# Ten raw weight tiles in place of eight, and another order of the seven block products in a two-layer trunk on one core

## Chip, core and metric

One Trainium2 chip, one core. The metric is the device time of one execution of the program in microseconds (us), where lower is better. The engines are TensorE (PE, matmuls), VectorE (DVE), ScalarE (ACT), GpSimd (POOL) and SyncE (SP, which here only issues DMAs). Each engine runs its own instructions in program order and waits on semaphores for the others.

## What is computed

The trunk has two layers on 256 tokens of width 2048, all in float32. The feed-forward half of each layer, where the change sits, is

```python
h = rms_norm(x, nw[2])
gate, up = jnp.split(h @ w_ffn_in[l], 2, axis=-1)      # 2048 x (2 * 5632)
x = x + rms_norm((jax.nn.silu(gate) * up) @ w_ffn_out[l], nw[3])
```

The other half projects `h` with `w_in` (2048 x 11264), runs a gated linear recurrence and a differential attention, projects both, merges them with sigmoid gates and projects again with `w_out`. Every weight is read once.

## The kernel before

**Weights.** Class `Weights` streams the weights as blocks of 256 x 512 float32 (512 KB). SP loads a block into a `w_raw` tile (L113). ACT casts it to the reduced type as `w_hi` (L130), and DVE forms the remainder `w_lo = w_raw - w_hi` (L131), called "the lo" of the block below. PE multiplies by each block three times (hi by the activations' hi, hi by their lo, lo by their hi): L365 to L367 in plain products, L454 to L456 in the fold groups. There are `RAW = 8` raw tiles, and `BUFS = 7` tiles each for hi and lo; conversion runs at most `LOOK = 5` blocks ahead of the block that PE asks for. A load is issued when a raw tile is free and at most `RAW - 1` blocks ahead of the block converted last.

**Fold groups.** Ten of the eleven 512-wide column pairs (gate, up) of each layer are computed by `fold_group`: for a 2 x 2 part of the blocks, seven products p1 to p7 stand in for eight, and the remaining blocks of both halves are multiplied plainly (A8, A10, A12, A14 for gate, B8 to B14 for up; "A12" is the block of rows 12 x 128 and following). Each product has two blocks, k0 and k1. The products need sums of weight blocks, made in place in the raw tiles: X starts as the block uA; after p1 has been converted, a DMA on POOL's queue adds uB to it from memory (`then`, L134, "X pair" for the two blocks), and p5 uses the sum. p6 adds Y on DVE (`plus`, L127), after which a second DMA pair adds uB to Y ("Y pair") for p7; p4 adds Z to X (`plus` again). So each group has four accumulating DMAs, 80 in all. Where such a DMA has not landed, the cast of the next use (p5 or p7) waits on ACT, and all of ACT's later casts behind it.

**Accumulators.** A fold group holds four PSUM tiles `s`, `b`, `c`, `d`, and there are only four, so that the next group's take over the same ones. `hold` (L1111, ACT) copies a finished `s`, `b` or `c` to SBUF: "hold p1", "hold p5", "hold u2", "hold p4". `out_a(0)` and `out_a(1)` (L1116, DVE) read `d` and `s` and give the gate; its sigmoid and product are L1092 (ACT) and L1093 (DVE). `out_b(0)` and `out_b(1)` (L1121, DVE) read `b` and `s` and give the up half, and L1096 (DVE) multiplies it in. PE's B8 for the second token tile writes `s` and so waits for `out_a(1)`; the next group's A8 writes what was `b` and waits for `out_b(0)`.

**Order.** The feed-forward is cut into four parts of 2, 3, 3 and 3 columns. In the first part one column is plain and one is a fold group ("alone" below, 2 in all); in the others each has three fold groups back to back, the first of which follows a plain stretch ("first", 6 in all) and the other two a fold group ("following", 12 in all). Between the parts come the plain products with `w_ffn_out`. While a group runs, the previous one's gated tile is transposed on PE (`hid`, L328 on DVE). PE runs its products in the order of the code. On DVE, ACT and SP the tile scheduler places each instruction, mostly by when the code asks for it. Within a group the blocks run in this order: p1 p1 A8 A10 p5 p5 p2 p2 p3 p3 p6 p6 A12 A14 p4 p4 p7 p7, then B8 B10 for the first token tile, B8 B10 for the second, B12 B14.

Of the kernel before, what the change touches and what calls it, by code (L numbers as in the profile page):

```python
# [12 lines left out]
F32 = mybir.dt.float32  # L13
F32R = mybir.dt.float32r
# [5 lines left out]
P = 128  # L20
# [6 lines left out]
NC = 512  # L27
KB = 2
# [40 lines left out]
class Weights:  # L69
# [2 lines left out]


    LOOK = 5
    RAW = 8
    BUFS = 7

    def __init__(self, nc, raw_pool, split_pool):
# [39 lines left out]
    def emit(self, upto):  # L118
        nc = self.nc
        upto = min(upto, self.oldest + self.BUFS - 1, len(self.order) - 1)  # L120
        while self.emitted <= upto:
            self.load(self.emitted)
            assert self.loaded > self.emitted
            key, _, plus, then, last = self.order[self.emitted]
            raw = self.raw[key]
            if plus is not None:
                nc.vector.tensor_tensor(raw, raw, self.raw[plus], op=ALU.add)  # L127
            hi = self.split_pool.tile([P, KB, NC], F32R, name="w_hi")
            lo = self.split_pool.tile([P, KB, NC], F32R, name="w_lo")
            nc.scalar.copy(hi, raw)  # L130
            nc.vector.tensor_tensor(lo, raw, hi.bitcast(F32), op=ALU.subtract)  # L131
            if then is not None:
                to, where = then
                nc.gpsimd.dma_start(self.raw[to], self.block(where), accum_op=ALU.add)  # L134
            for k in last if isinstance(last, tuple) else (key,) * last:
                del self.raw[k]
                self.live -= 1
            self.made[self.emitted] = (hi, lo)
            self.emitted += 1
            self.load(self.emitted + self.RAW - 1)  # L140

# [13 lines left out]
def hybrid_trunk(ctx: ExitStack, tc: tile.TileContext, ins, out):  # L155
# [22 lines left out]
        return work.tile([P, NC], F32, name=name, tag="w2")  # L178

    def stg_tile(name):  # L180
        return work.tile([P, NC], F32, name=name, tag="stg", bufs=7)

    def gate_tile(name):
        return work.tile([P, NC], F32, name=name, tag="stg", bufs=7)

    bg = Background()

# [222 lines left out]
    def fold_plan(src, nj, col_a, col_b, fold):  # L410
# [9 lines left out]
        ids = {}  # L420

        def through(col, ks):
            for k in ks:
                ids[col, k] = W.add(src=(src, k * P, col_a if col == "A" else col_b))
# [3 lines left out]
        through("A", plain[0:2])  # L428
        for i in n:
            ids["p5", i] = W.add(X[i], last=False)  # L430
        for i in n:
            ids["p2", i] = W.add(Z[i], dA[i], last=False)
        for i in n:
            ids["p3", i] = W.add(Y[i], dB[i], last=False)
        for i in n:
            ids["p6", i] = W.add(X[i], plus=Y[i], then=(Y[i], uB[i]), last=False)
        through("A", plain[2:])
        for i in n:
            ids["p4", i] = W.add(X[i], plus=Z[i], last=(X[i], Z[i]))
        for i in n:  # L440
# [4 lines left out]
    def fold_group(plan, lhs, hold, out_a, out_b):  # L445
# [12 lines left out]
        def folded(f, ps, first=False):  # L458
            for i in range(n):
                w = W.get(ids[f, i])  # L460
                for k in range(KB):
                    three(ps, lhs.factor[f, i, k], [s[:, k] for s in w], first and i == k == 0,
                          i == n - 1 and k == KB - 1)
                W.done(ids[f, i])
                bg.step()

        def through(col, k, ts, pss, first=False, done=True):
            w = W.get(ids[col, k])
            for t in ts:
                for i in range(KB):  # L470
                    three(pss[t], lhs.chunk(k + i, t), [s[:, i] for s in w], first and i == 0, i == KB - 1)
            if done:
                W.done(ids[col, k])
                bg.step()
# [4 lines left out]
            through("A", k, (0, 1), (d, c), m == 0)  # L479
        folded("p5", b, True)  # L480
        p5 = hold(b, 1.0)
        folded("p2", d)
        folded("p3", b)
        folded("p6", s)
        u2 = hold(s, 1.0)
        for k in plain[2:]:
            through("A", k, (0, 1), (d, c))
        out_a(0, p1, d, p1, ALU.add)
        folded("p4", c)
        p4 = hold(c, 1.0)  # L490
# [697 lines left out]
```

## Time and profile before

| what | value |
|---|---|
| median of 3 runs (lowest, highest) | 3014.52 us (3005.62, 3015.57) |
| the profiled execution, its span in the trace | 3015.97 us, 3014.2 us |
| PE busy | 2909.9 us, 97% of the span |
| DVE busy, ACT busy, POOL busy | 1936.3 us, 1451.9 us, 208.0 us |
| PE waiting for DVE at L454 (fold groups) | 75.6 us |
| bytes read from memory | 565.39 MB, 190 GB/s over the span |
| 20 fold groups in the trace | 945.7 us |

The profile is of one execution on the chip. "Busy" of PE counts a matmul's time whatever the clock, so a stretch at half clock looks as busy as one at full clock; the granted clock (1.00 is full speed) is read from the windows. A releaser in square brackets is what ended the idle time ahead of an instruction. DMA-issuing instructions of POOL stand as rows, and a DMA's landing is seen in who waited for it.

### The profile page before, as it was taken

Reading aid. Unit: us, or ns where it says so; the run is one execution under the profiler, and the core shown is the slowest. Engines: PE = TensorE matmul, PEld = TensorE weight load, DVE = VectorE, ACT = ScalarE, POOL = GpSimd, SP = SyncE. Lnnn points to the kernel's source line nnn. Section 1 sums busy time; section 2 is a strip of 40 time slices with the busy share of each in tenths; the row PEclk is TensorE's granted clock in tenths of the full one; section 3 lists DMA queues with packets and bytes.
Section 4 is the critical chain, followed back from the end, with each engine's and each line's share of the span. In section 5 each row is a group of like instructions: output and inputs, shape, how many; then the busy total and the mean of one; then the engine's idle time right before and its main releaser. Section 6 shows DMA issues by size and latency. Waiting matters only on the chain.

```text
span 3014.2 us, 35271 instructions
## 1 busy us (share of the span) xinstructions
PE 2909.9 (97%) x13194; PEld 2398.7 (80%) x13194; DVE 1936.3 (64%) x2098; ACT 1451.9 (48%) x1765; POOL 208.0 (7%) x236
## 2 busy tenths in 40 slices
PE   9999999999998998999999999999999999999988
PEld 7888888887786777877878888888877877777777
DVE  6676555555857667677666755455567676675775
ACT  6344544444655445455453444444445554454553
POOL 2002100000000000010000021000000010000000
PEclk9999999999999999999999999999999999999999
DMA  8555566665766776767665555666657767676674
GB/s 282 153 162 160 162 186 190 191 198 183 232 186 189 217 194 158 237 170 238 203 216 155 161 154 168 188 189 190 223 173 224 197 161 234 169 200 205 167 235 143
DMA packets 296315, 576.09 MB, mean 191 GB/s; under 512 B 18496, under 2 KB 18896, under 8 KB 296144
## 3 DMA queue, kind: packets, MB, share of 16 engines
q1 hardware_dynamic: 273232, 529.80, 55.3%
q0 software_dynamic: 21760, 41.95, 8.8%
q8 instruction: 103, 1.69, 0.2%
q10 hardware_dynamic: 1152, 2.10, 0.2%
q14 instruction: 68, 0.56, 0.1%
HBM read 565.39 MB, written 8.39 MB: 190 GB/s over the span
## 4 chain that ended last, share of the span: by engine, by line
PE 51%; issue 33%; DMA 8%; DVE 6%; ACT 1%; POOL 1%; POOLq 0%; SPq 0%; DVEq 0%; ACTq 0%
PE acc L365 13%; PE acc L367 13%; PE acc L366 13%; DMA w_raw<-in_w_ffn_in_dram 7%; DVE w_lo L131 4%; PE acc L454 3%; PE acc L455 3%; PE acc L456 3%; PE tp L630 2%; ACT w_hi L130 1%; PE tp L315 1%; DMA x_t<-in_x_dram 1%; POOL w_raw L134 1%; DVE w_raw L127 0%; DVE x_t L820 0%
## 5 line engine op out<-in xcount | busy, mean ns | idle before, releaser
L131 DVE TENSOR_TENSOR w_lo<-w_raw,w_hi 128x1024 fp32r<-128x1024 f32 x1128 | 1365.8, 1226 | 960.2 <-ACT w_hi L130 939.5
L130 ACT CAST w_hi<-w_raw 128x1024 fp32r<-128x1024 f32 x1128 | 1166.0, 1050 | 1357.1 <-PE acc L366 889.0
L365 PE MATMUL acc<-w_hi,xT 128*128 128x512 f32 x1536 | 616.7, 402 | 8.2 <-ACT w_hi L130 8.1
L367 PE MATMUL acc<-w_lo,xT 128*128 128x512 f32 x1536 | 603.5, 393 | 2.6 <-DVE w_lo L131 2.4
L366 PE MATMUL acc<-w_hi,xT 128*128 128x512 f32 x1536 | 601.5, 392 | 0.7 <-DVE xT L328 0.7
L454 PE MATMUL acc<-w_hi,xT 128*128 128x512 f32 x800 | 329.9, 412 | 75.5 <-DVE held L1116 44.7
L367 PEld LDWEIGHTS acc<-w_lo,xT 128*128 128x128 f32 x1536 | 289.9, 189 | 68.8 <-DVE w_lo L131 6.7
L365 PEld LDWEIGHTS acc<-w_hi,xT 128*128 128x128 f32 x1536 | 290.6, 189 | 65.6 <-ACT w_hi L130 9.8
L366 PEld LDWEIGHTS acc<-w_hi,xT 128*128 128x128 f32 x1536 | 290.9, 189 | 58.4 <-DVE xT L328 1.6
L455 PE MATMUL acc<-w_hi,xT 128*128 128x512 f32 x800 | 323.6, 405 | 0.0
L456 PE MATMUL acc<-w_lo,xT 128*128 128x512 f32 x800 | 323.0, 404 | 0.0
L366 PE MATMUL acc<-w_hi,hid 128*128 128x512 f32 x704 | 274.8, 390 | 0.0
L365 PE MATMUL acc<-w_hi,hid 128*128 128x512 f32 x704 | 274.4, 392 | 0.0
L367 PE MATMUL acc<-w_lo,hid 128*128 128x512 f32 x704 | 274.2, 390 | 0.0
L454 PEld LDWEIGHTS acc<-w_hi,xT 128*128 128x128 f32 x800 | 157.5, 197 | 122.1 <-DVE held L1116 52.7
L456 PEld LDWEIGHTS acc<-w_lo,xT 128*128 128x128 f32 x800 | 157.5, 197 | 34.9
L455 PEld LDWEIGHTS acc<-w_hi,xT 128*128 128x128 f32 x800 | 158.1, 198 | 32.5
L134 POOL DMA_DIRECT2D w_raw<-in_w_ffn_in_dram x80 | 97.5, 1219 | 1182.1 <-DVE w_lo L131 921.9
L366 PEld LDWEIGHTS acc<-w_hi,hid 128*128 128x128 f32 x704 | 132.2, 188 | 28.7 <-DVE hid L328 1.9
L367 PEld LDWEIGHTS acc<-w_lo,hid 128*128 128x128 f32 x704 | 132.1, 188 | 27.5
L365 PEld LDWEIGHTS acc<-w_hi,hid 128*128 128x128 f32 x704 | 132.2, 188 | 27.0
L454 PE MATMUL acc<-w_hi,fold_hi 128*128 128x512 f32 x320 | 125.7, 393 | 0.0
(204 smaller groups left out, 2920.9 us busy)
## 6 DMA issues: line engine op xcount, KB each, us to landing
w_raw<-in_w_in_dram SPq DMA_DIRECT2D x352, 512.0 KB, 3.8
w_raw<-in_w_ffn_in_dram SPq DMA_DIRECT2D x312, 512.0 KB, 4.8
w_raw<-in_w_ffn_out_dram SPq DMA_DIRECT2D x176, 512.0 KB, 4.8
w_raw<-in_w_ffn_in_dram POOLq DMA_DIRECT2D x80, 512.0 KB, 6.8
w_raw<-in_w_out_dram SPq DMA_DIRECT2D x64, 512.0 KB, 4.4
w_raw<-in_w_branch_a_dram SPq DMA_DIRECT2D x32, 512.0 KB, 3.6
w_raw<-in_w_branch_b_dram SPq DMA_DIRECT2D x32, 512.0 KB, 4.1
x_dram<-x_t SPq DMA_DIRECT2D x24, 256.0 KB, 5.5
```

The lines of the kernel that those rows point to most:

```text
L130: nc.scalar.copy(hi, raw)
L131: nc.vector.tensor_tensor(lo, raw, hi.bitcast(F32), op=ALU.subtract)
L134: nc.gpsimd.dma_start(self.raw[to], self.block(where), accum_op=ALU.add)
L315: nc.tensor.transpose(tp[:, i], src[:, i * P : (i + 1) * P], ident)
L365: nc.tensor.matmul(ps, xh, hi[:, j], start=first, stop=False)
L366: nc.tensor.matmul(ps, xl, hi[:, j], start=False, stop=False)
L367: nc.tensor.matmul(ps, xh, lo[:, j], start=False, stop=last)
L454: nc.tensor.matmul(ps, xh, hi, start=first, stop=False, skip_group_check=True)
L455: nc.tensor.matmul(ps, xl, hi, start=False, stop=False, skip_group_check=True)
L456: nc.tensor.matmul(ps, xh, lo, start=False, stop=last, skip_group_check=True)
L630: nc.tensor.matmul(ps[:, i, t], blk, right, start=True, stop=True)
```

## The change

There are ten raw tiles in place of eight. The room comes from the lo tiles (six in place of seven; the hi tiles stay seven) and from the tiles tagged `stg`, which hold the held and gated values (six in place of seven). In a fold group p2 moves from behind p5 to behind A14, and A12 moves from behind p6 to behind p5: p1 p1 A8 A10 p5 p5 A12 p3 p3 p6 p6 A14 p2 p2 p4 p4 p7 p7, and B as before. Lines behind the two functions move down by one or two: `hold` is L1113, `out_a` L1118, `out_b` L1123, the gated product L1098.

```diff
--- before.py
+++ after.py
@@ -72,7 +72,7 @@
 
 
     LOOK = 5
-    RAW = 8
+    RAW = 10
     BUFS = 7
 
     def __init__(self, nc, raw_pool, split_pool):
@@ -126,7 +126,7 @@
             if plus is not None:
                 nc.vector.tensor_tensor(raw, raw, self.raw[plus], op=ALU.add)
             hi = self.split_pool.tile([P, KB, NC], F32R, name="w_hi")
-            lo = self.split_pool.tile([P, KB, NC], F32R, name="w_lo")
+            lo = self.split_pool.tile([P, KB, NC], F32R, name="w_lo", bufs=self.BUFS - 1)
             nc.scalar.copy(hi, raw)
             nc.vector.tensor_tensor(lo, raw, hi.bitcast(F32), op=ALU.subtract)
             if then is not None:
@@ -178,10 +178,10 @@
         return work.tile([P, NC], F32, name=name, tag="w2")
 
     def stg_tile(name):
-        return work.tile([P, NC], F32, name=name, tag="stg", bufs=7)
+        return work.tile([P, NC], F32, name=name, tag="stg", bufs=6)
 
     def gate_tile(name):
-        return work.tile([P, NC], F32, name=name, tag="stg", bufs=7)
+        return work.tile([P, NC], F32, name=name, tag="stg", bufs=6)
 
     bg = Background()
 
@@ -428,13 +428,14 @@
         through("A", plain[0:2])
         for i in n:
             ids["p5", i] = W.add(X[i], last=False)
-        for i in n:
-            ids["p2", i] = W.add(Z[i], dA[i], last=False)
+        through("A", plain[2:3])
         for i in n:
             ids["p3", i] = W.add(Y[i], dB[i], last=False)
         for i in n:
             ids["p6", i] = W.add(X[i], plus=Y[i], then=(Y[i], uB[i]), last=False)
-        through("A", plain[2:])
+        through("A", plain[3:])
+        for i in n:
+            ids["p2", i] = W.add(Z[i], dA[i], last=False)
         for i in n:
             ids["p4", i] = W.add(X[i], plus=Z[i], last=(X[i], Z[i]))
         for i in n:
@@ -479,12 +480,13 @@
             through("A", k, (0, 1), (d, c), m == 0)
         folded("p5", b, True)
         p5 = hold(b, 1.0)
-        folded("p2", d)
+        through("A", plain[2], (0, 1), (d, c))
         folded("p3", b)
         folded("p6", s)
         u2 = hold(s, 1.0)
-        for k in plain[2:]:
+        for k in plain[3:]:
             through("A", k, (0, 1), (d, c))
+        folded("p2", d)
         out_a(0, p1, d, p1, ALU.add)
         folded("p4", c)
         p4 = hold(c, 1.0)
```

DVE, from the end of the fourth fold group to the first products of the fifth. In the list before, w_raw_8422 and 8424 are the new group's X blocks (so their first lo's are those of p1), and L1116 is the old group's `out_a(1)`:

```order
L131 TENSOR_TENSOR w_lo_8509<-w_raw_8409,w_hi_8508 128x1024
L131 TENSOR_TENSOR w_lo_8521<-w_raw_8422,w_hi_8520 128x1024
L131 TENSOR_TENSOR w_lo_8538<-w_raw_8424,w_hi_8537 128x1024
L1116 TENSOR_TENSOR held_8506<-held_8506,acc_8282 128x512
L131 TENSOR_TENSOR w_lo_8551<-w_raw_8436,w_hi_8550 128x1024
L1093 SCALAR_TENSOR_TENSOR held_8506<-held_8506,rs_5964,sgf_8534 128x512
L131 TENSOR_TENSOR w_lo_8573<-w_raw_8450,w_hi_8572 128x1024
```

and after, where 8417 and 8419 are the X blocks:

```order
L131 TENSOR_TENSOR w_lo_8513<-w_raw_8378,w_hi_8512 128x1024
L131 TENSOR_TENSOR w_lo_8523<-w_raw_8417,w_hi_8522 128x1024
L1118 TENSOR_TENSOR held_8510<-held_8510,acc_8284 128x512
L131 TENSOR_TENSOR w_lo_8538<-w_raw_8419,w_hi_8537 128x1024
L1095 SCALAR_TENSOR_TENSOR held_8510<-held_8510,rs_5966,sgf_8534 128x512
L131 TENSOR_TENSOR w_lo_8551<-w_raw_8432,w_hi_8550 128x1024
```

`out_a(1)` stood behind both lo's of the next p1, and now stands between them.

DVE, the rows that follow, from the second use of X (p5). Before, L1121 are `out_b(0)` and `out_b(1)` of the old group, 8498 and 8512 are Z (p2) and 8525 is the first Y block (p3):

```order
L131 TENSOR_TENSOR w_lo_8589<-w_raw_8422,w_hi_8588 128x1024
L127 TENSOR_TENSOR w_raw_8422<-w_raw_8422,w_raw_8525 128x1024
L131 TENSOR_TENSOR w_lo_8615<-w_raw_8424,w_hi_8614 128x1024
L1121 TENSOR_TENSOR held_8444<-acc_8283,held_8444 128x512
L127 TENSOR_TENSOR w_raw_8424<-w_raw_8424,w_raw_8542 128x1024
L1096 SCALAR_TENSOR_TENSOR held_8444<-held_8444,rs_5950,held_8308 128x512
L1121 TENSOR_TENSOR held_8364<-acc_8282,held_8364 128x512
L131 TENSOR_TENSOR w_lo_8627<-w_raw_8498,w_hi_8626 128x1024
L1096 SCALAR_TENSOR_TENSOR held_8364<-held_8364,rs_5964,held_8506 128x512
L131 TENSOR_TENSOR w_lo_8639<-w_raw_8512,w_hi_8638 128x1024
L131 TENSOR_TENSOR w_lo_8655<-w_raw_8525,w_hi_8654 128x1024
```

and after, where 8474 is A12's block and 8490 the first Y block:

```order
L131 TENSOR_TENSOR w_lo_8593<-w_raw_8417,w_hi_8592 128x1024
L127 TENSOR_TENSOR w_raw_8417<-w_raw_8417,w_raw_8490 128x1024
L1123 TENSOR_TENSOR held_8442<-acc_8285,held_8442 128x512
L1123 TENSOR_TENSOR held_8372<-acc_8284,held_8372 128x512
L1098 SCALAR_TENSOR_TENSOR held_8442<-held_8442,rs_5952,held_8308 128x512
L1098 SCALAR_TENSOR_TENSOR held_8372<-held_8372,rs_5966,held_8510 128x512
L131 TENSOR_TENSOR w_lo_8617<-w_raw_8419,w_hi_8616 128x1024
L131 TENSOR_TENSOR w_lo_8627<-w_raw_8474,w_hi_8626 128x1024
L131 TENSOR_TENSOR w_lo_8639<-w_raw_8490,w_hi_8638 128x1024
```

Both `out_b` stood behind the lo of p5's second block and now stand ahead of it; between that lo and p3's first there were seven instructions, and now there is one, A12's lo.

ACT in the fifth group, from p6 to p7. Before, L1111 held_8692 is hold p5 and held_8787 is hold u2; 8592 and 8618 are A12 and A14:

```order
L130 CAST w_hi_8681<-w_raw_8422 128x1024
L130 CAST w_hi_8695<-w_raw_8424 128x1024
L130 CAST w_hi_8714<-w_raw_8592 128x1024
L1111 ACTIVATE held_8692<-acc_8611 128x512
L130 CAST w_hi_8733<-w_raw_8618 128x1024
L327 CAST hid_8706<-tp_8707 128x4x128
L130 CAST w_hi_8746<-w_raw_8422 128x1024
L327 CAST hid_8706<-tp_8726 128x4x128
L130 CAST w_hi_8761<-w_raw_8424 128x1024
L130 CAST w_hi_8775<-w_raw_8525 128x1024
L1111 ACTIVATE held_8787<-acc_8610 128x512
L130 CAST w_hi_8789<-w_raw_8542 128x1024
```

and after, where 8542 is A14, 8554 and 8578 are Z (p2), held_8700 is hold p5 and held_8785 hold u2:

```order
L130 CAST w_hi_8687<-w_raw_8419 128x1024
L130 CAST w_hi_8702<-w_raw_8542 128x1024
L130 CAST w_hi_8728<-w_raw_8554 128x1024
L1113 ACTIVATE held_8700<-acc_8613 128x512
L130 CAST w_hi_8745<-w_raw_8578 128x1024
L327 CAST hid_8720<-tp_8721 128x4x128
L130 CAST w_hi_8756<-w_raw_8417 128x1024
L327 CAST hid_8720<-tp_8738 128x4x128
L130 CAST w_hi_8771<-w_raw_8419 128x1024
L130 CAST w_hi_8787<-w_raw_8490 128x1024
L130 CAST w_hi_8803<-w_raw_8502 128x1024
L1113 ACTIVATE held_8785<-acc_8612 128x512
```

Hold p5 stood behind A12's cast and now stands behind that of p2's first block; hold u2 stood ahead of the cast of p7's second block and now stands behind it.

At the program's start SP issues, before, three weight blocks, two tiles of x, six weight blocks, and the last tile of x; after, eight weight blocks stand ahead of that last tile of x in place of six. PE's products keep their order outside the fold groups.

## Rows read from the trace of the kernel before

**Rows 1.** The page, part 1: engine, busy us (share of the span), number of instructions.

```profile
PE 2909.9 (97%) x13194; PEld 2398.7 (80%) x13194; DVE 1936.3 (64%) x2098; ACT 1451.9 (48%) x1765; POOL 208.0 (7%) x236
```

**Rows 2.** PE's waits: instruction, what it waited for, us in total, times, longest.

```profile
PE acc L454 <- DVE held L1116: 44.7, 19, 4.9
PE acc L454 <- DVE held L1121: 26.8, 12, 4.4
PE acc L365 <- ACT w_hi L130: 8.1, 4, 2.2
PE acc L454 <- DVE hd L1096: 4.1, 2, 3.3
```

**Rows 3.** Timeline of PE: start, duration, line, in brackets idle time before and releaser.

```profile
1122.29 0.50 PE L454 MATMUL acc<-w_hi,xT 128*128 128x512 f32 x1 [3.19 <-DVE held L1116]
...
1138.72 0.50 PE L454 MATMUL acc<-w_hi,xT 128*128 128x512 f32 x1 [2.25 <-DVE held L1121]
```

**Rows 4.** Windows: length; PE, PEld, DVE, ACT, POOL busy (count); clock, DMA share, GB/s.

```profile
928.30:931.70 3.40, 3.37 (x8) 2.73 (x9) 3.40 (x4) 2.28 (x4) 0.00 (x0) 0.51 0.00 0
932.00:935.40 3.40, 3.40 (x16) 2.76 (x16) 3.40 (x4) 1.05 (x1) 0.25 (x1) 1.00 0.00 0
```

**Rows 5.** Line 134: duration in ns (min/median/max); its waiters (us, times); landing time.

```profile
L134 POOL DMA_DIRECT2D w_raw<-in_w_ffn_in_dram x80: 1203/1213/1381, 777.2 to 2907.2; - x80
...
  ACT w_hi L130: 211.1, 54
...
DMA to landing us min/median/max: 5.7/6.8/10.2
```

**Rows 6.** Timeline of ACT in the fifth group and the start of the sixth.

```profile
1135.76 3.90 ACT L130 CAST w_hi<-w_raw 128x1024 fp32r<-128x1024 f32 x4 [6.21 <-DMA w_raw<-in_w_ffn_in_dram]
...
1160.13 2.95 ACT L130 CAST w_hi<-w_raw 128x1024 fp32r<-128x1024 f32 x3 [2.00 <-DMA w_raw<-in_w_ffn_in_dram]
...
1185.16 3.89 ACT L130 CAST w_hi<-w_raw 128x1024 fp32r<-128x1024 f32 x4 [7.51 <-DMA w_raw<-in_w_ffn_in_dram]
```

**Rows 7.** Timeline of DVE in the same stretch (x4: four instructions in a row).

```profile
1136.84 1.23 DVE L131 TENSOR_TENSOR w_lo<-w_raw,w_hi 128x1024 fp32r<-128x1024 f32 x1 [4.77 <-ACT w_hi L130]
1137.99 0.68 DVE L1121 TENSOR_TENSOR held<-acc,held 128x512 f32<-128x512 f32 x1
...
1142.78 4.62 DVE L131 TENSOR_TENSOR w_lo<-w_raw,w_hi 128x1024 fp32r<-128x1024 f32 x4
```

**Rows 8.** Timeline of POOL in the same stretch: the accumulating DMAs.

```profile
1145.55 1.21 POOL L134 DMA_DIRECT2D w_raw<-in_w_ffn_in_dram  x1 [15.60 <-DVE w_lo L131]
1151.77 1.22 POOL L134 DMA_DIRECT2D w_raw<-in_w_ffn_in_dram  x1 [5.01 <-DVE hid L328]
1169.82 1.21 POOL L134 DMA_DIRECT2D w_raw<-in_w_ffn_in_dram  x1 [16.83 <-DVE w_lo L131]
```

**Rows 9.** Windows over the twelve following groups: the third of them, and the sum.

```profile
1132.23:1179.48 47.25, 43.97 (x189) 35.57 (x188) 35.71 (x36) 26.26 (x30) 4.87 (x4) 0.96 0.71 198
...
sum 586.48, PE 531.61 PEld 429.91 DVE 442.79 ACT 321.31 POOL 43.84; mean PE 44.30 PEld 35.83 DVE 36.90 ACT 26.78 POOL 3.65
```

**Rows 10.** The same over the six first groups: the second, the third, and the sum.

```profile
1086.30:1132.23 45.93, 42.74 (x182) 34.84 (x180) 33.97 (x32) 25.29 (x28) 4.87 (x4) 0.96 0.71 199
1295.43:1336.90 41.47, 41.09 (x181) 33.71 (x180) 34.07 (x32) 24.89 (x28) 4.84 (x4) 1.00 0.76 217
...
sum 267.42, PE 252.54 PEld 206.35 DVE 198.38 ACT 153.11 POOL 29.14; mean PE 42.09 PEld 34.39 DVE 33.06 ACT 25.52 POOL 4.86
```

**Rows 11.** The same over the two groups that stand alone: the first, and the sum.

```profile
787.55:832.46 44.91, 42.37 (x189) 34.42 (x188) 35.60 (x35) 27.32 (x31) 2.43 (x2) 1.00 0.72 220
...
sum 91.80, PE 86.00 PEld 70.05 DVE 73.16 ACT 54.63 POOL 4.85; mean PE 43.00 PEld 35.03 DVE 36.58 ACT 27.32 POOL 2.43
```

**Rows 12.** The start: timeline of PE, and a window over all engines.

```profile
22.84 0.63 PE L315 MATMUL tp<-ident,x_t 128*128 128x128 f32 x4 [0.96 <-DMA x_t<-in_x_dram]
...
8.00:22.00 14.00, 12.98 (x52) 9.57 (x52) 11.73 (x11) 8.58 (x11) 8.24 (x5) 1.00 1.03 372
```

## The prediction

> **What bounds the kernel now.** I read the page first: PE is busy 97% of the span [rows 1], so only its idle time and its slow time can be won. The view of PE's waits says where the idle time is: 44.7 us at L454 for L1116 in 19 waits and 26.8 us for L1121 in 12, and 4.1 us for the gated product [rows 2]. That is 75.6 us, all in the fold groups, and all for DVE. The timeline shows one of each: PE stands 3.19 us for `out_a(1)` and 2.25 us for `out_b(0)` [rows 3]. A wait costs more than its idle time: after one, 3.4 us run at clock 0.51 (the lower of the two levels, 1.2 GHz), with 8 matmuls where the next window has 16 at full clock [rows 4], so some 1.7 us are lost on top.
>
> DVE has no lack of time (64% busy [rows 1]), so the next question is what makes it late. Line 134's view answers: ACT waited 211.1 us in 54 waits for accumulating DMAs, which land 6.8 us after their issue in the median (5.7 to 10.2) [rows 5]. ACT is in order, so all later casts stand behind such a wait, and all of DVE's lo's behind the casts.
>
> The three timelines of the fifth and sixth group give a closed loop, from p5's second cast to the same cast one group later [rows 6 to 8]:
> (a) that cast starts at 1135.76; DVE forms its lo at 1136.84, then goes through `out_b` and its company from 1137.99 to 1142.78, then four lo's 1.14 apart, of which the second is p3's first, done at 1142.78 + 2 x 1.14 = 1145.06: 9.3 us.
> (b) The Y pair, issued at 1145.55 and, as the second goes out only when the first has landed, at 1151.77; the cast of p7's second block starts at 1160.13: 15.1 us.
> (c) Casts and lo's up to p1's first of the next group, whose X pair POOL issues at 1169.82, 0.45 us behind the lo's end: 9.2 us.
> (d) The X pair, until p5's second cast at 1185.16: 15.8 us.
> The sum is 49.4 us, and the twelve following groups last 586.48 / 12 = 48.87 us each [rows 9]. PE alone would need less: the third of the first groups ran at clock 1.00 almost without waits and took 41.47 us for its 180 matmuls, 0.23 each [rows 10]; eight transposes more raise PE's busy time from 41.09 to 42.37 us [rows 10, 11], so a following group needs between 41.5 and 42.7. Hence the loop is what sets the twelve groups' length, and PE's two waits are how it shows.
>
> **Following groups (twelve).** The new order takes six instructions from between the lo's of p5k1 and p3k0: both `out_b`, both gated products and one `plus` go ahead of p5k1's lo or behind p3k0's (the lists of DVE), and p2's two lo's give way to A12's one. Those ahead fill the time in which DVE waits for the X pair anyway (4.77 us idle there [rows 7], against 2.5 us of work). Part (a) becomes 1.08 us from cast to lo plus three lo's of 1.14, 4.5 us in place of 9.3, so 4.8 us less. Parts (b), (c), (d) hold the same instructions as before, so I leave them. The mean goes from 48.87 to 44.1 us, still above PE's 42.7 at most. Twelve times 4.8 is **57.6 us**. What is late next is the same loop, so I expect a wait of some 2 us per group at `out_a(1)` to stay, and the one at `out_b` to go, since `out_b` no longer stands behind a lo that waits for an accumulating DMA.
>
> **First groups (six).** They come to 267.42 us, or 44.6 each [rows 10], without part (d). Between the lo's of p5k1 and p3k0 stand two additions of the size of L1121's (0.6 us apart from the next row, 1137.99 [rows 7]), a `plus` as long as a lo, and p2's two lo's; A12's lo alone remains, which brings the Y pair forward by 3.5 us, and `out_a(1)` is one lo (1.14) earlier besides. Together 4.6 us against a wait of 3.19 us in the group shown [rows 3]; so I let the waits go and take 41.7 us, just above the undisturbed 41.47: 6 x 2.9 = **17 us**. The bounds are nothing, if these waits hang on something other than the lo's, and 18.6 us.
>
> **Groups alone (two).** 91.80 us [rows 11]; PE's own 42.4 each would save 7.0. Their wait for the gated product goes, since these too stand ahead of p5k1's lo. I take **7 us**, between 0 and 7.
>
> **Tiles.** Six lo tiles make DVE wait for the product six blocks back where the hi tiles wait for the seventh. In plain stretches a block is converted some five blocks ahead, so at most one block's PE time (2.8 us, 12 matmuls of 0.23) of a lead of some 14 us is lost; I cost it at nothing, covered by that lead. It moves the X pair of a first group some 1.6 us later, which lands before p5 all the same. Six tiles for held and gated values: four are live in a group and two wait for their transposes, so six do; nothing, and if a release came late it would hold ACT's hold, with casts queued behind it.
>
> **Start.** Ten tiles let SP issue two more weight loads ahead of the last tile of x. PE waits 0.96 us for that tile already [rows 12], and the DMA engines are full, at 372 GB/s; two loads of 524 KB take 1.05 MB / 372 GB/s = 2.8 us, all of it on the path: **+2.8 us**, with bounds of 0 and 3.
>
> **New waits.** On ACT, hold p5 now stands behind the cast of p2's first block, which waits for PE to finish p5 (seven hi tiles) and for the sums X += Y. By the first it ends 48 matmuls into the group, 11.0 us, plus a cast and the hold: 12.7 us. By the second, counting DVE's rows, it ends 10.3 us after p5k1's cast. PE writes the same accumulator again with p3, 60 matmuls or 13.8 us into the group, so hold p5 costs nothing while p5k1's cast starts within 3.5 us of the group's start; in the fifth group that was 1135.76 - 1132.23 = 3.5 us [rows 6, 9], and it should come down with part (a). I take nothing, with 0 to 2.2 us per group (the sixth group's cast, at 1185.16, came 5.7 us after its start). Hold u2, now behind the cast that waits for the Y pair, is needed only by p7, which needs that pair itself; nothing.
>
> **Sum.** The profiled execution took 3015.97 us, 1.45 us above the median of three. 3016.0 - 57.6 - 17.2 - 7.0 + 2.8 = 2937.
>
> A rule that bears on parts (b) and (d): the rows give 5.7 us at least from issue to landing for 512 KB [rows 5]. The Trainium skill, page "DMA: Bandwidth & Descriptors", section "Anatomy of one DMA — SWDGE (gpsimd) path", fits 2.0 us plus bytes over 436e3, an estimate of 3.2 us here. By that a pair would take about 7 us, the loop 33 before the change, PE would be the bound already, and the change would gain nothing in the following groups. The trace disagrees, as ACT's 54 waits show, and the sum goes by the trace.
>
> **Rivals.**
> 1. *All waits in the fold groups go.* This happens if the pairs get shorter too, as loads come earlier with ten tiles and leave the accumulating DMAs alone. For it: a landing of 5.7 us was seen; four of these in place of 6.8 take 4.4 us off the loop, down to 39.7, under PE. Against: loads go on at about 198 GB/s all through [rows 9]. Following groups 12 x (48.87 - 42.4) = 77.6, the others 18.6 + 7.0, start 2.8: 2916; with PE's 8.1 us of waits for hi in plain stretches [rows 2] gone as well, 2908.
> 2. *Part of the gain is taken back.* One landing of the four at 10.2 us in place of 6.8 makes the loop 47.5 us: 12 x 1.4 = 16 us in place of 57.6, so 2978. Or hold p5 becomes the late one: 2.2 us in each of twelve, 26 us, so 2963.
> 3. *Slower.* Ten tiles let SP put two more loads beside each accumulating DMA, and all four land at 10.2 us. A pair then takes 0.45 + 2 x 10.2 + 0.3 = 21.2 us, the loop 4.5 + 9.2 + 42.4 = 56.1, and 12 x 7.2 = 87 us are added; less the 24 us of the other groups, plus the start, 3082. The point from which this decides is where (b) and (d) together grow by more than the 4.8 us that (a) loses, from 30.9 to 35.7, plus 2 us for the other groups' gain. Against it: loads keep to PE's pace, and at 198 GB/s are far from the 372 GB/s of the start.
> 4. *The change doesn't do what it says.* If Y's own load came late, p3's lo would wait for it whatever the order, and nothing would move: about 3010 to 3020.
>
> **How the numbers follow.** The forecast has 0.60, rival 1 has 0.12, rival 2 has 0.18, rival 3 has 0.06, rival 4 has 0.04. The range goes from 2908 (rival 1) to 2978 (rival 2) and leaves out rivals 3 and 4 and the tails. About 0.3%, 9 us, is what a measurement of this kernel can tell from no change. Faster takes the first three, 0.90; same is rival 4, 0.04; slower rival 3, 0.06.
>
> **What would show it.** In the profile after: waits for `out_b` (L1123) near zero, and for `out_a` (L1118) below 40 us in total; following groups of 43 to 45 us; about 4.5 us from p5k1's cast to p3k0's lo; pairs still of about 15 us; some 3.8 us of wait for the last tile of x. If pairs come out at 13 or at 18 us, rival 1 or 2 holds; if the first wait in a group is of p3 for L1113, hold p5 is the cause. I am wrong if the groups' length is not set by the loop: if part (a) shrinks and the length stays.

## The result and the profile after

The changed kernel takes 2928.65 us (median of 4 runs, 2923.34 to 2930.42) against 3015.05 us for the kernel before (4 runs), a ratio of 0.9715 (95% interval 0.9689 to 0.9741). The forecast was 2937, with a range of 2908 to 2978. So the time lies in the range, 8 us below the forecast. The profiled execution has a span of 2921.6 us in place of 3014.2.

PE's waits in the changed kernel (what for, us in total, times, longest us), against [rows 2]:

```profile
PE acc L455 <- ACT held L1113: 13.5, 12, 2.2
...
PE tp L315 <- DMA x_t<-in_x_dram: 5.2, 2, 3.6
...
PE acc L455 <- DVE held L1118: 0.8, 2, 0.6
```

The waits for `out_b` (L1121 before, L1123 now) and for the gated product are gone, as is all but 0.8 us of those for `out_a`. New are twelve waits for a hold on ACT (L1113), as many as there are following groups.

The windows over the groups (length, busy times, clock): the third of the twelve following groups and their sum, the second of the six first groups and their sum, and the sum of the two alone, to be set against [rows 9 to 11]:

```profile
1113.37:1157.13 43.76, 42.01 (x189) 34.60 (x188) 37.43 (x38) 26.24 (x30) 4.87 (x4) 1.00 0.80 217
...
sum 517.90, PE 504.41 PEld 415.06 DVE 445.43 ACT 321.74 POOL 45.60; mean PE 42.03 PEld 34.59 DVE 37.12 ACT 26.81 POOL 3.80
```

```profile
1072.57:1113.37 40.80, 40.80 (x181) 33.80 (x180) 32.45 (x32) 25.86 (x28) 4.87 (x4) 1.00 0.80 230
...
sum 246.25, PE 245.44 PEld 202.59 DVE 195.21 ACT 155.06 POOL 27.39; mean PE 40.91 PEld 33.76 DVE 32.53 ACT 25.84 POOL 4.56
```

```profile
sum 83.84, PE 83.75 PEld 69.17 DVE 74.34 ACT 54.30 POOL 4.94; mean PE 41.87 PEld 34.59 DVE 37.17 ACT 27.15 POOL 2.47
```

The twenty groups take 517.9 + 246.3 + 83.8 = 848.0 us in place of 945.7, so 97.7 us less; the span fell by 92.6. The start takes 2.7 us back (below); the 2.4 that are left lie elsewhere, and what they went to is not shown. The clock is 1.00 in every one of the twenty windows; before it was 0.93 to 0.97 in all the following groups. A first group without waits takes 40.80 us, with PE busy in all of it.

What sets the following groups now is seen in the fifth and sixth group. ACT:

```profile
1118.88 3.90 ACT L130 CAST w_hi<-w_raw 128x1024 fp32r<-128x1024 f32 x4 [6.19 <-DMA w_raw<-in_w_ffn_in_dram]
...
1125.84 2.95 ACT L130 CAST w_hi<-w_raw 128x1024 fp32r<-128x1024 f32 x3 [1.63 <-DVE w_raw L127]
1128.69 0.59 ACT L1113 ACTIVATE held<-acc 128x512 f32<-128x512 f32 x1
...
1137.20 1.06 ACT L130 CAST w_hi<-w_raw 128x1024 fp32r<-128x1024 f32 x1 [2.12 <-DMA w_raw<-in_w_ffn_in_dram]
...
1162.49 3.90 ACT L130 CAST w_hi<-w_raw 128x1024 fp32r<-128x1024 f32 x4 [6.98 <-DMA w_raw<-in_w_ffn_in_dram]
```

DVE, POOL and PE in the same stretch:

```profile
1115.12 1.28 DVE L1123 TENSOR_TENSOR held<-acc,held 128x512 f32<-128x512 f32 x2
...
1119.96 4.63 DVE L131 TENSOR_TENSOR w_lo<-w_raw,w_hi 128x1024 fp32r<-128x1024 f32 x4 [2.23 <-ACT w_hi L130]
```

```profile
1123.88 1.21 POOL L134 DMA_DIRECT2D w_raw<-in_w_ffn_in_dram  x1 [10.80 <-DVE w_lo L131]
1130.10 1.22 POOL L134 DMA_DIRECT2D w_raw<-in_w_ffn_in_dram  x1 [5.01 <-ACT held L1113]
1147.32 1.21 POOL L134 DMA_DIRECT2D w_raw<-in_w_ffn_in_dram  x1 [16.00 <-DVE w_lo L131]
```

```profile
1129.33 0.50 PE L455 MATMUL acc<-w_hi,fold_hi 128*128 128x512 f32 x1 [1.75 <-ACT held L1113]
```

Both `out_b` (1115.12) now run while DVE waits for p5's second block (1119.96), as forecast. The Y pair goes out at 1123.88, 5.0 us after p5k1's cast at 1118.88; before it was 9.8 us (1135.76 to 1145.55, [rows 6, 8]). But hold p5 (1128.69) stands behind three casts, the first of which waited for the sum X += Y until 1125.84, and PE's p3 starts at 1129.33, 1.75 us late. The Y pair sets nothing any more: its cast at 1137.20 waits 2.12 us on ACT, and no wait of PE comes of that.

A loop still sets the length, but another one, and hold p5 is no part of it. What closes it is DVE's own work, from the lo of p5's second block to the end of the next p1's first lo, behind which the X pair goes out. This stretch of the fifth group as a window (start:end, length; PE, PEld, DVE, ACT, POOL busy; clock, DMA share, GB/s), after and then before:

```profile
1119.96:1146.91 26.95, 25.20 (x115) 20.70 (x114) 26.70 (x26) 21.92 (x26) 2.44 (x2) 1.00 0.79 230
```

```profile
1136.84:1169.37 32.53, 30.65 (x132) 25.18 (x133) 29.17 (x30) 21.57 (x26) 2.44 (x2) 0.95 0.67 197
```

Before, DVE stood still for 32.53 - 29.17 = 3.4 us of it, waiting for ACT's casts, 2.1 us of it for the one that waits for the Y pair (1160.13, [rows 6]). After, it has four instructions fewer in the stretch, both `out_b` and their products, and stands still for 0.25 us, although PE stands for 1.75. So the loop is 1.1 us from p5's cast to its lo, 26.9 of DVE's work, and 15.6 until the X pair is in and p5's cast of the sixth group starts (1162.49): 43.6 in all. PE needs 41.74 us for such a group (e9 below), so it has to wait somewhere in each, and does so at hold p5. In the other five places where a third group follows a second, DVE stands still for 0.2 to 1.2 us of the stretch. From a first group to a second it is 2.0 to 4.1 us, for PE's matmuls and for casts, so that there DVE alone does not close the loop.

### The profile page after: what moved, and what is told of

The parts are those of the page before. It is cut to its first block, busy times and chain, and to the rows that moved or that the text cites. A ratio compares the mean times of both kernels' runs of the same rounds, so it can differ in the third digit from the quotient of the medians.

```text
span 2921.6 us, 35664 instructions
## 1 busy us (share of the span) xinstructions
PE 2873.0 (98%) x13194; PEld 2378.0 (81%) x13194; DVE 1944.5 (67%) x2098; ACT 1453.5 (50%) x1765; POOL 206.4 (7%) x236
## 5 line engine op out<-in xcount | busy, mean ns | idle before, releaser
L365 PE MATMUL acc<-w_hi,xT 128*128 128x512 f32 x1536 | 616.1, 401 | 9.4 <-ACT w_hi L130 8.1
L367 PE MATMUL acc<-w_lo,xT 128*128 128x512 f32 x1536 | 602.9, 393 | 2.8 <-DVE w_lo L131 2.6
L366 PE MATMUL acc<-w_hi,xT 128*128 128x512 f32 x1536 | 601.2, 391 | 0.7 <-DVE xT L328 0.7
L367 PEld LDWEIGHTS acc<-w_lo,xT 128*128 128x128 f32 x1536 | 289.7, 189 | 68.8 <-DVE w_lo L131 7.0
L365 PEld LDWEIGHTS acc<-w_hi,xT 128*128 128x128 f32 x1536 | 290.2, 189 | 67.1 <-ACT w_hi L130 9.8
L366 PEld LDWEIGHTS acc<-w_hi,xT 128*128 128x128 f32 x1536 | 290.6, 189 | 58.5 <-DVE xT L328 1.6
L455 PE MATMUL acc<-w_hi,xT 128*128 128x512 f32 x800 | 311.7, 390 | 0.8 <-DVE held L1118 0.8
L457 PE MATMUL acc<-w_lo,xT 128*128 128x512 f32 x800 | 311.3, 389 | 0.0
L456 PE MATMUL acc<-w_hi,xT 128*128 128x512 f32 x800 | 311.3, 389 | 0.0
L455 PEld LDWEIGHTS acc<-w_hi,xT 128*128 128x128 f32 x800 | 150.2, 188 | 33.2 <-DVE held L1118 1.8
L457 PEld LDWEIGHTS acc<-w_lo,xT 128*128 128x128 f32 x800 | 150.2, 188 | 31.3
L456 PEld LDWEIGHTS acc<-w_hi,xT 128*128 128x128 f32 x800 | 150.2, 188 | 31.0
L455 PE MATMUL acc<-w_hi,fold_hi 128*128 128x512 f32 x320 | 127.4, 398 | 13.6 <-ACT held L1113 13.5
```

The costliest lines, as they stand in the source:

```text
L365: nc.tensor.matmul(ps, xh, hi[:, j], start=first, stop=False)
L366: nc.tensor.matmul(ps, xl, hi[:, j], start=False, stop=False)
L367: nc.tensor.matmul(ps, xh, lo[:, j], start=False, stop=last)
L455: nc.tensor.matmul(ps, xh, hi, start=first, stop=False, skip_group_check=True)
L456: nc.tensor.matmul(ps, xl, hi, start=False, stop=False, skip_group_check=True)
L457: nc.tensor.matmul(ps, xh, lo, start=False, stop=last, skip_group_check=True)
```

## The experiments

The runs were made in sets, each on one chip, and the kernel before did not take the same time on all: in the median 2986 us beside e1 to e4 (chip 11 in the record), 2984 beside e9, e4 again and the changed kernel a third time (chip 6), and 3013 beside e5, e6 and the changed kernel again (chip 10). For the result above, with 3015, no chip is on record. Each ratio is therefore to the kernel before in the same set; the last section shows what differs.

**Tiles alone (e1).**

```diff
-    RAW = 8
+    RAW = 10
-            lo = self.split_pool.tile([P, KB, NC], F32R, name="w_lo")
+            lo = self.split_pool.tile([P, KB, NC], F32R, name="w_lo", bufs=self.BUFS - 1)
-        return work.tile([P, NC], F32, name=name, tag="stg", bufs=7)
+        return work.tile([P, NC], F32, name=name, tag="stg", bufs=6)
```

> The kernel before with the tiles of the change alone: ten raw tiles, six lo tiles, six held and gated tiles, the old order of the products. If the order made the gain (the loop through the two accumulating pairs was shortened), this gains nothing: 3012 to 3022 us, PE's waits for out_a and out_b (L1116, L1121) 65 to 78 us in total as before, and 2.7 us more of wait for the last tile of x at the start. If the two more raw tiles made the gain, because loads come earlier: 2925 to 2970 us, with those waits below 30 us.

Measured: 2938.18 us against 2986.43, ratio 0.9839 (0.9814 to 0.9865). My theory, by which the order made the gain, falls here. Time and waits lie where the other theory, earlier loads by more raw tiles, put them; that the raw tiles are not the reason either comes out in e5 and e6. All waits for `out_b` are gone; of those for `out_a` this is left:

```profile
PE acc L454 <- DVE held L1116: 15.9, 12, 3.5
```

**Order alone (e2).** The changed kernel with `RAW = 8`, seven lo tiles and seven held and gated tiles.

> The changed kernel with the old tiles: eight raw, seven lo, seven held and gated tiles, the new order of the products. If the order made the gain: 2921 to 2930 us, about 2.7 us less than the changed kernel from the start, with some 13 us of waits of PE for hold p5. If the new order needs the ten tiles (Y's or Z's loads come late with eight), the casts of p3 or p2 wait for loads, and the time lies at 2950 us or above.

Measured: 2971.16 us against 2986.43, ratio 0.9951 (0.9937 to 0.9965), in the place where the second theory put it, but not for its reason: the casts of p3 do not wait for loads. PE waits for `out_b` as before, and hardly for `out_a`:

```profile
PE acc L455 <- DVE held L1123: 36.4, 12, 4.5
...
PE acc L455 <- DVE held L1118: 4.3, 5, 1.3
```

So the order of the products cures `out_a`, and something in the tiles cures `out_b`. DVE's rows in e2 say why: with seven lo tiles both `out_b` (L1123) still stand behind the lo of p5's second block, the first right behind it:

```profile
1123.31 1.23 DVE L131 TENSOR_TENSOR w_lo<-w_raw,w_hi 128x1024 fp32r<-128x1024 f32 x1 [5.60 <-ACT w_hi L130]
1124.46 0.68 DVE L1123 TENSOR_TENSOR held<-acc,held 128x512 f32<-128x512 f32 x1
```

That they move ahead of it comes with the tiles.

**Six lo tiles alone (e5), and the changed kernel with eight raw tiles (e6).** The first is the kernel before with this one edit:

```diff
-            lo = self.split_pool.tile([P, KB, NC], F32R, name="w_lo")
+            lo = self.split_pool.tile([P, KB, NC], F32R, name="w_lo", bufs=self.BUFS - 1)
```

The second is the changed kernel with two edits undone:

```diff
-    RAW = 10
+    RAW = 8
-        return work.tile([P, NC], F32, name=name, tag="stg", bufs=6)
+        return work.tile([P, NC], F32, name=name, tag="stg", bufs=7)
```

> The kernel before with six lo tiles in place of seven, nothing else. In the program, this alone puts DVE's instructions into the same order as all the changed tiles together do (out_b ahead of the lo of p5's second block, out_a ahead of the lo of p1's second block). If that order is what gained in the run with the changed tiles alone, the ratio to the kernel before is 0.980 to 0.986 here too. If the ten raw tiles gained there, by earlier loads, the ratio here is 0.993 or above.

> The changed kernel with eight raw tiles and seven held and gated tiles, six lo tiles and the new order of products. DVE and ACT have the very order of the changed kernel. If the ten raw tiles are worth nothing in the fold groups, this is 2 to 4 us faster than the changed kernel, by the start alone. If they let loads come earlier and that counts, it is more than 5 us slower.

Measured, beside a kernel before of 3012.83 us: e5 2953.54 us, ratio 0.9801 (0.9778 to 0.9824); e6 2926.42 us, ratio 0.9714 (0.9693 to 0.9734). The changed kernel itself in the same set:

> The changed kernel once more, beside the experiments. If the time of its following groups is set by hold p5 behind the X pair, landings of 6.3 us in place of 6.9 take 1.2 us off these groups, down to PE's own 41.7 at least: 0.978 to 0.982 of the kernel before where that takes 2986 us, that is 2920 to 2932.

Measured: 2931.10 us, ratio 0.973 (0.971 to 0.9749). So taking one tile of 512 KB away is worth 59 us by itself, and no gain is seen from the two more raw tiles (and one held tile fewer, which e6 undoes with them). Without them the median is 4.7 us lower, of which the start explains 2.4 (PE waits 2.5 us for x in place of 4.9), and the runs of the two overlap. In e5 the waits for `out_b` are gone and those for `out_a` stay, as in e1; DVE's rows, where both `out_b` (L1121) stand ahead of the lo of p5's second block, then PE's waits, then the sums over the following and the first groups:

```profile
1124.64 1.28 DVE L1121 TENSOR_TENSOR held<-acc,held 128x512 f32<-128x512 f32 x2
...
1129.68 4.63 DVE L131 TENSOR_TENSOR w_lo<-w_raw,w_hi 128x1024 fp32r<-128x1024 f32 x4 [2.44 <-ACT w_hi L130]
```

```profile
PE acc L454 <- DVE held L1116: 34.6, 19, 3.5
```

```profile
sum 529.13, PE 509.61 PEld 416.32 DVE 439.80 ACT 316.36 POOL 43.85; mean PE 42.47 PEld 34.69 DVE 36.65 ACT 26.36 POOL 3.65
```

```profile
sum 264.94, PE 253.62 PEld 206.59 DVE 199.08 ACT 152.20 POOL 29.14; mean PE 42.27 PEld 34.43 DVE 33.18 ACT 25.37 POOL 4.86
```

A following group takes 529.13 / 12 = 44.1 us there, in place of 48.9 in the kernel before of that set, and a first group 44.2, where the kernel before has 43.8: the tile helps the following groups and not the first. (The execution profiled took 2962.53 us, 9 us more than the median of e5.) In e6, which has the new order too, PE's waits are those of the changed kernel but for the start:

```profile
PE acc L455 <- ACT held L1113: 16.3, 14, 2.6
...
PE tp L315 <- DMA x_t<-in_x_dram: 2.5, 2, 1.5
```

**More space for descriptors (e3).** The kernel before, with

```diff
-                    dynamic_dma_scratch_size=1024)
+                    dynamic_dma_scratch_size=2048)
```

> The kernel before with twice the scratch space for the descriptors of POOL's DMAs (2048 bytes per partition in place of 1024), nothing else. In the trace of before the second accumulating DMA of a pair is issued only 0.3 us after the first has landed. If it waits there for room for its descriptors, a pair now takes 9 to 11 us in place of 15, the loop goes from 49.4 to 38 to 41 us, PE sets the length of the groups, and the time is 2920 to 2950 us in the old order. If the second DMA waits for something else, or if the two together are no faster than one after the other, pairs stay at 14 to 16 us and the time at 3010 to 3020 us.

Measured: 2919.58 us against 2986.43, ratio 0.9787 (0.9755 to 0.9818). The changed kernel was not run in that set; in the others it took 2928 to 2931. POOL's timeline shows the two accumulating DMAs of a pair go out one right behind the other (x2); then line 134's landing time, PE's waits, and the sum over the following groups:

```profile
2573.07 2.47 POOL L134 DMA_DIRECT2D w_raw<-in_w_ffn_in_dram  x2 [21.02 <-DVE w_lo L131]
```

```profile
DMA to landing us min/median/max: 5.5/6.4/12.4
```

```profile
PE acc L454 <- DVE held L1121: 6.8, 6, 1.8
PE acc L454 <- DVE held L1116: 4.9, 9, 0.6
```

```profile
sum 518.54, PE 506.83 PEld 413.35 DVE 443.50 ACT 320.18 POOL 44.24; mean PE 42.24 PEld 34.45 DVE 36.96 ACT 26.68 POOL 3.69
```

So the second DMA did wait for descriptor space: in all 40 pairs of the kernel before it goes out 0.3 us after the first has landed, in all 40 here 2.8 to 7.0 us ahead of that. And the pairs are what set the groups' length: with nothing else touched, in the old order and with seven lo tiles, the following groups fall to 518.54 / 12 = 43.2 us. The size was less than expected: side by side the slower of the two takes up to 12.4 us, and in the mean an X pair takes 12.1 us and a Y pair 12.9 (from the lo's end to the cast, over the twelve groups), not 9 to 11; in a profile of the kernel before from the same set, the last one below, they take 14.7 and 15.0.

**Hold p5 earlier (e4, twice).** The changed kernel, where the cast of p6's second block is asked for one block later and pinned behind the hold:

```diff
             for i in range(n):
+                W.look = W.LOOK - (f == "p5" and i == n - 1)
                 w = W.get(ids[f, i])
+                W.look = W.LOOK
...
         p5 = hold(b, 1.0)
+        W.pin = tc.keep_in_program_order
```

> The changed kernel, with hold p5 issued on ACT ahead of the cast of p6's second block in place of behind the cast of p2's first block. If the place of hold p5 on ACT is what PE's 13.5 us of waits for L1113 come from, these fall below 3 us, the following groups last 41.5 to 42.2 us, and the time is 2913 to 2919 us. If the accumulating pairs are the bound behind it, the wait comes back elsewhere (at p7 for the Y pair, at out_a, or at p5 for the X pair), and the time stays within 4 us of the changed kernel's 2929.

> The changed kernel with hold p5 issued earlier on ACT, once more, beside the changed kernel itself on the same chip. If hold p5's place on ACT cost its 13 to 16 us of waits and nothing else is late behind it, this is 10 to 14 us faster than the changed kernel. The first run of it showed 11.1 us of waits for out_a in place of those for hold p5, at 42.99 us per following group; if that is the same loop through the X pair, come out at another place, the gain over the changed kernel is 0 to 8 us.

> The changed kernel, beside the two others on the same chip: 0.970 to 0.975 of the kernel before if that takes 3005 to 3020 us here; where the accumulating DMAs land in 6.3 us in place of 6.8 and the kernel before takes 2986, 0.977 to 0.982.

Measured: 2922.95 us both times, ratios 0.9795 (0.9768 to 0.9821) and 0.9796 (0.9777 to 0.9814); the changed kernel beside the second 2928.22 us, ratio 0.9814 (0.9798 to 0.983). The gain is 5 us and not 10 to 14 (and in the first run the time lay 6 us from 2929, not within 4). The wait did come back elsewhere, at `out_a` (L1125 in this kernel), and the following groups take 516.14 / 12 = 43.0 us in place of 522.19 / 12 = 43.5; e4's row and sum of the second run, then the changed kernel's:

```profile
PE acc L459 <- DVE held L1125: 12.9, 12, 2.6
```

```profile
sum 516.14, PE 504.51 PEld 413.90 DVE 447.60 ACT 316.86 POOL 44.59; mean PE 42.04 PEld 34.49 DVE 37.30 ACT 26.41 POOL 3.72
```

```profile
PE acc L455 <- ACT held L1113: 14.9, 11, 2.4
```

```profile
sum 522.19, PE 506.27 PEld 416.16 DVE 443.75 ACT 320.68 POOL 44.03; mean PE 42.19 PEld 34.68 DVE 36.98 ACT 26.72 POOL 3.67
```

The stretch of DVE's work in the fifth group of the second run shows why:

```profile
1116.53:1144.30 27.77, 27.77 (x128) 23.00 (x127) 26.56 (x26) 21.84 (x26) 2.44 (x2) 1.00 0.75 220
```

PE stands nowhere in it now, and it is no shorter, since DVE is busy for 26.6 us of it, where it was 26.7. So hold p5 is only where the loop through DVE and the X pair comes out; to move it moves the place.

**Order, six lo tiles and descriptor space (e9).** e6 with 2048 bytes for the descriptors.

> New order of products and six lo tiles, with eight raw and seven held and gated tiles, and twice the scratch space for the descriptors of POOL's DMAs (2048 in place of 1024 bytes per partition). With that space the kernel before had X pairs of 12.1 us in place of 14.6 and Y pairs of 12.9 in place of 15.6 in the mean. Taken off the loop of the changed kernel, whose following groups last 43.2 to 43.6 us and need 41.7 of PE, they leave PE as the bound: no wait for hold p5, out_a or out_b above 3 us in total, following groups 41.7, first ones 40.8, 829 us for all twenty in place of 855, and 0.961 to 0.967 of the kernel before (2897 to 2913 us where that takes 3013). If two accumulating DMAs side by side slow the loads that the new order needs early (Y behind A12), waits for loads at p3 appear and the ratio is 0.970 or above.

Measured: 2901.70 us (2900.97 to 2902.46) against 2984.37, ratio 0.9724 (0.9708 to 0.974), 26.5 us faster than the changed kernel beside it and the fastest of all. The time lies where it was expected; the ratio does not, as the kernel before took 2984 and not 3013 in that set. The first of PE's waits, then the sums over following and first groups:

```profile
PE acc L365 <- ACT w_hi L130: 8.1, 4, 2.2
PE acc L367 <- DVE w_lo L131: 3.3, 7, 0.6
```

```profile
sum 500.89, PE 500.89 PEld 414.90 DVE 445.61 ACT 326.69 POOL 43.63; mean PE 41.74 PEld 34.58 DVE 37.13 ACT 27.22 POOL 3.64
```

```profile
sum 244.80, PE 244.80 PEld 202.74 DVE 196.00 ACT 152.04 POOL 28.98; mean PE 40.80 PEld 33.79 DVE 32.67 ACT 25.34 POOL 4.83
```

No wait of the fold groups is left in that list, and PE is busy for the whole of every group: 41.74 us for a following one, 40.80 for a first, and 829 us for all twenty, as expected. An X pair takes 11.1 us in the mean, so the loop would need 1.1 + 26.9 + 11.1 = 39.1 us, less than PE: what is left there is PE's own time. What the order and the lo tile each still add with this descriptor space was not run apart.

## Why the prediction was right, and where it was not

**What bounds the kernel: right.** The closed loop through two accumulating pairs was read off three timelines; e3 shortened the pairs alone, with DVE's and ACT's instructions in the same order, and the groups followed.

**What moves DVE's instructions: wrong.** The prediction said that the new order takes six instructions from between p5's second lo and p3's first, and costed the tiles at nothing. In the runs the order alone gives 15 us and leaves `out_b` behind p5's lo, with 36.4 us of waits (e2); six lo tiles alone give 59 us in the other set (e5), and in the program they put `out_b` ahead of it and leave four lo's up to p3's first, some 5.7 us from p5's cast in place of 9.3. The new order then takes one more lo away. The step that failed is a reading of the two lists of DVE as the effect of one edit, where four edits had gone into the second list (three kinds of tiles and the order). That the missing lo tile makes the scheduler place a lo later, behind `out_b`, is what fits; shown is only that the one tile suffices for DVE's whole order: the lists of e5 and of e1 are the same row by row, as are those of e6 and the changed kernel, and so is the order of DVE's 2098 instructions in their traces.

**Following groups: mis-sized.** 57.6 us were forecast and 586.5 - 517.9 = 68.6 came. Part (a) shrank as said (Y pair 5.0 us after p5's cast in place of 9.8), but the loop with 44.1 us was not the one that ended up binding. The step that was mis-sized is "Parts (b), (c), (d) hold the same instructions as before, so I leave them." The Y pair dropped out of the loop, and DVE's own work took its place: from p3's first lo to the next p1's first, (b) and (c) had 24.3 us, and the fifth group now takes 43.6 - 4.5 - 15.6 = 23.5. The mean came to 43.2 us. In all, the groups gave 97.7 us where 81.8 were forecast, every term too small.

**A wait of 2 us at `out_a` to stay: wrong place.** It was at hold p5, for which I had taken nothing, with a bound of 2.2 us per group; it is 13.5 / 12 = 1.1. The sign that I gave, "if the first wait in a group is of p3 for L1113, hold p5 is the cause", came and misled: hold p5 is where PE waits, and e4 shows that it does not set the groups' length. The condition that I gave for the wait decided: hold p5 costs nothing while p5's second cast starts within 3.5 us of the group's start, and in the fifth group it started at 1118.88 - 1113.37 = 5.5. That this cast "should come down with part (a)" was the error: PE's part of the group shrank, while the X pair before the cast stayed at 15 us.

**First and single groups: right, with a floor set too high.** 17.2 and 7.0 us were forecast, 267.4 - 246.3 = 21.2 and 8.0 came. A first group takes 40.80 us, and the row of 41.47 that I used still held a wait. These 21 us are not to be had everywhere: in the last profile of the kernel before (below), on another chip, its first groups have no such waits.

**Start: right.** PE waits 3.65 us for the last tile of x in place of 0.96 [rows 12], 2.7 us more; 2.8 was the estimate:

```profile
25.30 0.63 PE L315 MATMUL tp<-ident,x_t 128*128 128x128 f32 x4 [3.65 <-DMA x_t<-in_x_dram]
```

**Rivals.** That accumulating DMAs get slower beside more loads did not happen; they land as before, and ACT waits as long for them:

```profile
  ACT w_hi L130: 213.1, 51
...
DMA to landing us min/median/max: 5.7/6.9/8.8
```

That they get faster did not happen either. The estimate of 3.2 us by the Trainium skill (page "DMA: Bandwidth & Descriptors", section "Anatomy of one DMA — SWDGE (gpsimd) path") lies below every landing in these runs, of which the shortest took 5.4 us (e2). The sum came out near the time although its reasons named the wrong edit, because it was made on DVE's list of the whole changed kernel.

## What to carry to other kernels

When a change has several edits, ask of each alone what it does to the order of instructions, before the trace is read for what that order costs: here the edit that looked like a mere price for the others (one lo tile fewer) made most of the gain, and the one that it paid for (two raw tiles more) made none. Where a closed loop sets the time, to take a wait away at one exit of it moves the wait to the next. Look for the members of the loop that are busy or under way all through it, here DVE's 27 us of work and a pair of DMAs that ran one after the other for want of descriptor space, and shorten one of these.

## What the runs showed of the hardware

Two DMAs issued by POOL, of 512 KB each, ran one behind the other with 1024 bytes of descriptor space and side by side with 2048. The gain was far less than half a pair (X pairs 12.1 us in place of 14.7 in the mean, e3), since side by side the slower one took up to 12.4 us in place of 10.2.

The kernel before had two times, 3013 to 3015 and 2984 to 2986 us, in different sets of runs (medians), while the changed kernel took 2928 to 2931 in both. Two more profiles of the kernel before, with what was expected of each:

> The kernel before once more, for a trace beside those of the experiments. The experiments so far saw the accumulating DMAs land in 6.2 to 6.4 us in the median, where the first traces had 6.8 and 6.9, and the kernel before took 2986 us there in place of 3015. If the landing time is what differs between the two, a landing 0.5 us shorter in four DMAs takes 2 us off the loop of each of twelve groups, 24 us in all: the following groups last about 47 us here in place of 48.9, with the same two waits (L1116, L1121).

> The kernel before once more. It took 3013 to 3015 us in two sets of runs and 2984 to 2986 us in two others, while the changed kernel took 2928 to 2931 in all. If this run is of the faster sort, its trace says what differs: if landings of the accumulating DMAs are shorter, the pairs take 14 us or less in the mean in place of 14.6 and 15.6, and the following groups last 46 to 47.5 us in place of 48.9; if instead the clock is granted differently after the same waits, the pairs are as long as before and only PE's half-clock windows are fewer. If it is of the slower sort, groups of 48.8 us come out again and the question stays open.

The first of them ran on chip 10 and took 3014.40 us (landing 6.8 us in the median, following groups 586.20 us in all), so it answered nothing. The second ran on chip 5, took 2984.35 us (another execution beside it 2977.29) and shows the difference: the landing of the accumulating DMAs, PE's waits, the sums over following and first groups, and SP's queue on the page, of which the last row is the same line of the kernel before as first profiled:

```profile
DMA to landing us min/median/max: 5.5/6.3/9.2
```

```profile
PE acc L454 <- DVE held L1121: 34.5, 12, 3.8
PE acc L454 <- DVE held L1116: 16.8, 13, 2.8
```

```profile
sum 577.63, PE 527.63 PEld 427.19 DVE 440.58 ACT 321.36 POOL 43.85; mean PE 43.97 PEld 35.60 DVE 36.72 ACT 26.78 POOL 3.65
```

```profile
sum 244.97, PE 244.97 PEld 202.61 DVE 199.70 ACT 149.67 POOL 29.14; mean PE 40.83 PEld 33.77 DVE 33.28 ACT 24.94 POOL 4.86
```

```profile
q1 hardware_dynamic: 273232, 529.80, 52.8%
```

```profile
q1 hardware_dynamic: 273232, 529.80, 55.3%
```

The same packets took 0.528 x 2982.6 = 1575 us of the engines' time in place of 0.553 x 3014.2 = 1667, 5.5% less, and the accumulating DMAs landed 0.5 us sooner. But neither forecast came out: the X pairs took 14.7 us in the mean, as before (14.6), and the Y pairs 15.0 in place of 15.6, so the following groups gained little (8.9 us, to 48.1 us each). The first groups gained 22.5 us: their Y pairs took 14.4 us in the mean in place of 16.2, their waits for `out_a` went altogether, and with them the stretches at half clock. In the changed kernel the same packets differed too (57.0% of 2921.6 us, and 54.0% of 2926.3 on chip 6, which is 5.1% less) and its time did not: its X pairs took 14.8 and 15.0 us. So a few per cent of DMA speed moved the time only where they removed a wait of PE. The gain of the change is 2.7 to 2.9% in the sets of 3013 to 3015 us and 1.9% on chip 6. As each set ran on a chip of its own, it is likely but not shown that the chip makes the difference, and why the DMA engines differ stays open. So does why the changed kernel's accumulating DMAs landed in 6.7 us on chip 6, where those of e4 landed in 6.0.
